# Forgetting attention: six heads' probabilities turned by VectorE and two transfers instead of by TensorE

## The chip, the cores and the metric

The kernel runs on one core of a Trainium2 chip. The metric is the device time of one execution in microseconds. Engines in the profile: PE (TensorE matmuls) and PEld (its weight loads), DVE (VectorE), ACT (ScalarE), POOL (GpSimd), SP (the queue that issues most transfers).

## The reference

A trunk of two layers over 256 tokens of width 1024, all in float32. Each layer has a half-step SwiGLU block, a token mixer, another half-step SwiGLU block, and a gated embedding. The mixer of layer 0 is a latent attention; that of layer 1, which the change concerns, is a forgetting attention with eight heads of 128:

```python
def fox_mixer(u, w_in, b_f, w_o):
    q, k, v, f_logit = jnp.split(u @ w_in, [hd, 2 * hd, 3 * hd], axis=-1)
    log_f = jax.nn.log_sigmoid(f_logit + b_f)
    cum = jnp.cumsum(log_f, axis=1).transpose(0, 2, 1)
    # per block of 128 queries [q0, q1), keys [0, q1):
    s = einsum('bqhd,bkhd->bhqk', q, k) * scale + cum[query] - cum[key]
    probs = softmax(where(k_pos <= q_pos, s, NEG_INF))
    o = einsum('bhqk,bkhd->bqhd', probs, v)
    return o.reshape(b, s, hd) @ w_o
```

With 256 tokens there are two blocks of queries; the first sees 128 keys, the second 256. So a head has three squares of 128x128 probabilities.

## The kernel before

Everything is written in an order fixed by hand; each engine runs its instructions in that order and waits for others by semaphores. The stream of the residual stands as `hT`, features on partitions and tokens along the row. Products with weights run in halves of float32: the class `Weights` fetches raw weight blocks of 512 KB in the order of a plan (`fetch`, L92, issued on SP's queue, four raw buffers), ScalarE makes the high half (`high`, L101) and VectorE the low half (`low`, L105), after which the raw buffer is free and SP may issue the next fetch. `part` (L252, L253) multiplies such a block.

`fox` first makes the values `v` for all heads, then calls `attention` with a lag of 2. The loop there runs over steps h = 0 to 9, and in step h it does, in this order:

- `shares(h - 2)`: VectorE scales the probabilities of head h-2 by the inverse of their sum (L525 to L527); then `low()` makes low halves of earlier outputs (L233);
- `project(h, 0)`: TensorE multiplies a weight block for queries (eight pairs of L252 and L253), VectorE scales it out of PSUM (L857), GpSimd adds the halves, then `W.pump()` runs one L105 and so frees a raw buffer;
- `turn(h - 2)`: TensorE transposes the three squares of probabilities into PSUM (L533), ScalarE copies them to `ptS` (L535);
- `scores(h - 1)`: TensorE (L864, L867), then VectorE's masked maxima (L506) and ScalarE's exponentials (L518, L519);
- `project(h, 1)`: the same for keys (VectorE adds, L858);
- `values(h - 2)`: TensorE multiplies `ptS` and `v` (L540, L541), ScalarE copies to `os` (L542).

From step 8 on there is nothing to project, and `fill_some` puts in pairs of the output projection, as many as `FOX_FILLS` says (4, 7, 6, 5), over the heads that `ready` counts as done. The tile `kqv` is shared by both attentions; the forgetting attention uses 16 of the 24 blocks of its part `kq`.

Of the kernel before, what the change touches and what calls it, by code (L numbers as in the profile page):

```python
# [11 lines left out]
F32 = mybir.dt.float32  # L12
# [7 lines left out]
P = 128  # L20
D = 1024
T = 256
# [3 lines left out]
H = 8  # L26
# [5 lines left out]
FOX_SCALE = 128.0 ** -0.5  # L32
# [16 lines left out]
FOX_FILLS = {(8, 0): 4, (8, 1): 7, (9, 0): 6, (9, 1): 5}  # L49
# [95 lines left out]
def trunk(ctx, tc, xT, xt, pT, pos, freq, bf, lead0, lead1, ffn_in, ffn_out, w_down, w_uq, w_ukv, mla_o,  # L145
          fox_qk, fox_v, fox_o, ple_gate, ple_proj, ple_rows, gain_row, out):
    nc = tc.nc
# [4 lines left out]
    work = ctx.enter_context(tc.tile_pool(name="work", bufs=2))  # L152
    psum = ctx.enter_context(tc.tile_pool(name="psum", bufs=7, space=bass.MemoryType.PSUM))
    dram = ctx.enter_context(tc.tile_pool(name="dram", bufs=1, space=bass.MemoryType.DRAM))
# [45 lines left out]
    ready = const.tile([P, 2], F32, name="ready")  # L200
# [21 lines left out]
    def bank(name, shape=(P, 2, T)):  # L222
        return psum.tile(list(shape), F32, name=name, tag="mm")
# [8 lines left out]
    def rest(hi, lo, src):  # L232
        nc.vector.tensor_sub(lo, src, hi.bitcast(F32))  # L233
# [21 lines left out]
    def parts(ps):  # L255
        return [ps] if len(ps.shape) == 2 else [ps[:, 0, :], ps[:, 1, :]]
# [232 lines left out]
            pass  # L489


    def attention(project, score, v, mask, scale, nxt, lag, fills, early, cumq=None):
        late = lag > 2
        os = act.tile([P, H, 2, T], F32R, name="os", tag="u")
        probs = {}
        turned = {}
        lows = []

        def scores(h):
            ps = bank("psc", (P, 3 * P))  # L500
            score(h, (ps[:, :P], ps[:, P:]))
            m = work.tile([P, 2], F32, name="m", bufs=3)
            pr = work.tile([P, 3 * P], F32, name="pr", bufs=4)

            for i, a in enumerate((slice(0, P), slice(P, 3 * P))):
                nc.vector.tensor_tensor_reduce(pr[:, a], ps[:, a], mask[:, P - i * P:], 1.0, NEG, op0=ALU.add,  # L506
                                               op1=ALU.max, accum_out=m[:, i:i + 1])
            nm = work.tile([P, 2], F32, name="nm", bufs=3)
            if cumq is None:
                nc.vector.scalar_tensor_tensor(nm, m, -1.0, scale, op0=ALU.mult, op1=ALU.mult)  # L510
                by = scale[:, 0:1], scale[:, 1:2]
            else:
                by = scale, scale
                top = work.tile([P, 2], F32, name="top", bufs=3)
                nc.vector.scalar_tensor_tensor(top, m, scale, cumq[:, h, :], op0=ALU.mult, op1=ALU.add)
                nc.vector.tensor_sub(nm, cumq[:, h, :], top)
            den = work.tile([P, 2], F32, name="den", bufs=3)
            nc.scalar.activation(pr[:, :P], pr[:, :P], AF.Exp, bias=nm[:, 0:1], scale=by[0], accum_out=den[:, 0:1])  # L518
            nc.scalar.activation(pr[:, P:], pr[:, P:], AF.Exp, bias=nm[:, 1:2], scale=by[1], accum_out=den[:, 1:2])  # L519
            probs[h] = pr, den  # L520

        def shares(h):
            pr, den = probs[h]
            inv = work.tile([P, 2], F32, name="inv", bufs=3)
            nc.vector.reciprocal(inv, den)  # L525
            nc.vector.tensor_scalar(pr[:, :P], pr[:, :P], inv[:, 0:1], None, op0=ALU.mult)
            nc.vector.tensor_scalar(pr[:, P:], pr[:, P:], inv[:, 1:2], None, op0=ALU.mult)  # L527

        def turn(h):
            pr, _ = probs.pop(h)  # L530
            pt = bank("pt", (P, 3 * P))
            for i in range(3):
                nc.tensor.transpose(pt[:, i * P:(i + 1) * P], pr[:, i * P:(i + 1) * P], ident)  # L533
            turned[h] = work.tile([P, 3 * P], F32, name="ptS", bufs=3)
            nc.scalar.activation(turned[h], pt, AF.Copy)  # L535

        def values(h):
            p = turned.pop(h)
            po = bank("po", (P, T))
            nc.tensor.matmul(po, v[:, 0, h * P:(h + 1) * P], p[:, :T], start=True, stop=False)  # L540
            nc.tensor.matmul(po[:, P:], v[:, 1, h * P:(h + 1) * P], p[:, T:], start=False, stop=True)  # L541
            nc.scalar.activation(os[:, h, 0, :], po, AF.Copy)  # L542
            lows.append((os[:, h, 0, :], os[:, h, 1, :], po))

        def low():

            while lows:
                rest(*lows.pop())


        ws, pss, upto = {}, {}, {}
        ready = 0

        def fill(d, n):
            if d not in ws:
                ws[d], = W.get()

                pss[d] = bank("ps2", (P, 2, T) if d < KD - 3 else (P, T))
            if upto.setdefault(d, 0) < n:
                part(pss[d], ws[d], os, range(upto[d], n), H - 1)  # L560
                upto[d] = n

        def fill_some(n):
            while n > 0:
                d = min(ws, key=lambda d: (upto[d], d), default=None)
                if d is None or upto[d] >= ready:
                    if len(ws) == early:
                        return
                    d = len(ws)
                    upto[d] = 0  # L570
                m = min(ready - upto[d], n)
                if m <= 0:
                    return
                fill(d, upto[d] + m)
                n -= m

        def finish(d):
            W.done(ws[d])
            src = hT[:, d, :]
            for p in parts(pss[d]):  # L580
                nc.vector.tensor_add(src, p, src)
            if d >= KD - 2:
                nxt.last(d, src)
                if d == KD - 1:
                    W.pump(2)
                return
            nxt.high(d, src)
            if d < early and d:
                nxt.low(d - 1, hT[:, d - 1, :])
            if d >= early - 1:  # L590
                W.pump()
                nxt.low(d, src)
            nxt.square(src)

        for h in range(H + lag):
            if 0 <= h - 2 < H:
                shares(h - 2)
            low()
            if h == H and not late:
                W.pump()  # L600
            if late:

                ready = h - lag - 1
            if h < H:
                project(h, 0)
            fill_some(fills.get((h, 0), 0))
            if 0 <= h - lag:
                turn(h - lag)
            if late and h in MLA_HIGHS:
                W.begin()  # L610
            if 0 <= h - 1 < H:
                scores(h - 1)
            if h < H:
                project(h, 1)
            if not late:
                W.catch_up()
            elif h in MLA_LOWS:
                W.pump(ahead=0)
            ready = h - lag - late
            fill_some(fills.get((h, 1), 0))  # L620
            if 0 <= h - lag:
                values(h - lag)
            if h >= H and not late:
                W.catch_up()
        low()
        for n in (H - 1, H):
            for d in range(early):
                fill(d, n)
                if n == H:
                    finish(d)  # L630
        for d in range(early, KD):
            fill(d, H)
            finish(d)

    def keys_values():

        kqv = big.tile([P, 2 * KF, T], F32, name="kqv", tag="big")
        return kqv[:, :24, :], kqv[:, 24:32, :].rearrange("p (t c) n -> p t (c n)", t=2), kqv[:, 32:34, :]
# [130 lines left out]
    def fox(norm, nxt):  # L769
        kq, v, _ = keys_values()  # L770
# [3 lines left out]
        cumq = work.tile([P, H, 2], F32, name="cumq", bufs=1)  # L774
# [45 lines left out]
        for c in range(3):  # L820
# [22 lines left out]
            for t in range(2):  # L843
                r = norm.rtok[:, t:t + 1]
# [6 lines left out]
        def project(h, half):  # L851
# [7 lines left out]
            if (h, half) != (H - 1, 1):  # L859
                W.pump()  # L860

        def score(h, dst):
            for t in range(2):
                nc.tensor.matmul(dst[t], kq[:, 2 * h, t * P:(t + 1) * P], kq[:, 2 * h + 1, :(t + 1) * P],  # L864
                                 start=t == 0, stop=False)
            for t in range(2):
                nc.tensor.matmul(dst[t], pick[:, h:h + 1].to_broadcast([G, P]), drop[:, :(t + 1) * P],  # L867
                                 start=False, stop=t == 1)

        attention(project, score, v, cmask[:, 1, :], FOX_SCALE, nxt, 2, FOX_FILLS, 4, cumq=cumq)  # L870


    class Embedding:
# [198 lines left out]
    for k in range(KD):  # L1072
        if k % 2 == 0:
            hi, lo = W.pair()
        c = slice(k % 2 * 4 * P, (k % 2 + 1) * 4 * P)
        n0.high(k, steps[:, k, :T], vector=k == 0)

        n = 4 * P if k else 2 * P
# [33 lines left out]
    cmask = const.tile([P, 2, 2 * P], BF16, name="cmask")  # L1112
# [103 lines left out]
    for i in range(2):  # L1216
# [6 lines left out]
        p = Embedding(i)  # L1223
# [91 lines left out]
```

## Time and profile before

| | |
|---|---|
| median of 3 runs | 988.9 us (988.71 to 989.48) |
| span of the profiled execution, first to last instruction | 987.5 us |
| TensorE, VectorE, ScalarE, GpSimd busy | 99%, 74%, 52%, 43% of the span |
| granted TensorE clock, mean | 0.998 |
| memory read | 179.65 MB, 183 GB/s over the span |
| the eight steps with projections in the forgetting attention | about 686 to 741 us |
| shares of the core's transfer engines there | 0.44 to 0.77 busy |

A span is not quite an execution's own time: 988.9 as measured against 987.5 here, and the 1.4 us around the span hold no instruction of the engines. In rows of a timeline the columns are start, duration (both in us), engine, line, operation, output and inputs, size, count, and in brackets the idle time before it and what ended it. TensorE's matmuls are pipelined, so a pitch is read from start to start, not from a duration. "To landing" is the time from the issue of a transfer to its completion.

### The profile page before, as it was taken

Reading aid. Unit: us, or ns where it says so; the run is one execution under the profiler, and the core shown is the slowest. Engines: PE = TensorE matmul, PEld = TensorE weight load, DVE = VectorE, ACT = ScalarE, POOL = GpSimd, SP = SyncE. Lnnn points to the kernel's source line nnn. Section 1 sums busy time; section 2 is a strip of 40 time slices with the busy share of each in tenths; the row PEclk is TensorE's granted clock in tenths of the full one; section 3 lists DMA queues with packets and bytes.
Section 4 is the critical chain, followed back from the end, with each engine's and each line's share of the span. In section 5 each row is a group of like instructions: output and inputs, shape, how many; then the busy total and the mean of one; then the engine's idle time right before and its main releaser. Section 6 shows DMA issues by size and latency. Waiting matters only on the chain.

```text
span 987.5 us, 15908 instructions
## 1 busy us (share of the span) xinstructions
PE 978.5 (99%) x5800; PEld 863.9 (87%) x5800; DVE 734.1 (74%) x1101; ACT 510.6 (52%) x802; POOL 423.7 (43%) x359
## 2 busy tenths in 40 slices
PE   9999999999999999999999999999999999999997
PEld 7888888998988888889888888899889888888886
DVE  6777879686858777667877886667877677786685
ACT  7555444466545554545555544546445555554361
POOL 0777731110357775111477772211221377772010
PEclk9999999999999999999999999999999999999999
DMA  8576666573456666665376665657543556666582
GB/s 326 184 253 206 200 176 198 176 209 108 147 148 208 209 210 177 203 194 185 115 209 208 195 185 178 187 178 231 157 138 101 197 182 208 209 190 199 138 278 58
DMA packets 62622, 184.11 MB, mean 186 GB/s; under 512 B 15148, under 2 KB 16816, under 8 KB 62416
## 3 DMA queue, kind: packets, MB, share of 16 engines
q1 hardware_dynamic: 61616, 181.58, 59.6%
q8 instruction: 46, 0.75, 0.3%
q10 hardware_dynamic: 576, 0.85, 0.3%
q0 software_dynamic: 352, 0.66, 0.3%
q14 instruction: 32, 0.26, 0.1%
HBM read 179.65 MB, written 1.05 MB: 183 GB/s over the span
## 4 chain that ended last, share of the span: by engine, by line
PE 94%; DVE 3%; ACT 1%; DMA 1%; issue 1%; POOL 0%; POOLq 0%; SPq 0%; ACTq 0%; DVEq 0%
PE po L252 17%; PE pu L252 16%; PE pg L252 16%; PE po L253 8%; PE pg L253 8%; PE pu L253 8%; PE ps L252 5%; PE ps L253 2%; PE ps L237 2%; PE ps L239 2%; PE ps L238 2%; DVE wlo L105 1%; PE pv L237 1%; PE pv L239 1%; PE pv L238 1%; PE po L540 1%
## 5 line engine op out<-in xcount | busy, mean ns | idle before, releaser
L105 DVE TENSOR_TENSOR wlo<-raw,whi 128x1024 fp32r<-128x1024 f32 (+2 forms) x339 | 416.2, 1235 | 28.3 <-ACT whi L101 28.1
L101 ACT ACTIVATE whi<-raw 128x1024 fp32r<-128x1024 f32 (+2 forms) x339 | 336.2, 1023 | 38.8 <-DMA raw<-in_ffn_in_dram 16.4
L395 POOL TENSOR_TENSOR gu<-two 128x256 f32<-128x256 f32 x176 | 216.7, 1232 | 114.2 <-DVE two L393 107.6
L252 PE MATMUL pg<-u,whi 128*128 128x512 f32 x702 | 251.0, 395 | 0.2 <-DVE u L297 0.2
L252 PE MATMUL pu<-u,whi 128*128 128x512 f32 x702 | 250.9, 395 | 0.1
L252 PE MATMUL po<-hs,whi 128*128 128x512 f32 x704 | 246.8, 394 | 0.0
L253 PE MATMUL pg<-u,wlo 128*128 128x256 f32 x702 | 197.1, 281 | 0.6 <-DVE wlo L105 0.4
L253 PE MATMUL po<-hs,wlo 128*128 128x256 f32 x704 | 197.2, 280 | 0.0
L253 PE MATMUL pu<-u,wlo 128*128 128x256 f32 x702 | 196.8, 280 | 0.0
L252 PEld LDWEIGHTS po<-hs,whi 128*128 128x128 f32 x704 | 132.2, 188 | 31.3
L252 PEld LDWEIGHTS pu<-u,whi 128*128 128x128 f32 x702 | 131.8, 188 | 31.3 <-issue 0.4
L252 PEld LDWEIGHTS pg<-u,whi 128*128 128x128 f32 x702 | 131.8, 188 | 31.1 <-ACT whi L1080 0.3
L253 PEld LDWEIGHTS pg<-u,wlo 128*128 128x128 f32 x702 | 132.0, 188 | 1.6 <-DVE wlo L105 1.1
L253 PEld LDWEIGHTS po<-hs,wlo 128*128 128x128 f32 x704 | 132.3, 188 | 0.0
L253 PEld LDWEIGHTS pu<-u,wlo 128*128 128x128 f32 x702 | 132.0, 188 | 0.1
L413 POOL TENSOR_TENSOR hid<-sg,gu 128x256 f32<-128x256 f32 x88 | 122.1, 1387 | 6.9
L308 POOL TENSOR_TENSOR acc<-acc,sq 128x256 f32<-128x256 f32 x42 | 43.3, 1031 | 177.7 <-ACT sq L303 155.0
L229 ACT ACTIVATE hs<-hid 128x256 fp32r<-128x256 f32 x88 | 36.8, 418 | 155.2 <-POOL hid L413 153.1
L233 DVE TENSOR_TENSOR hs<-hid,hs 128x256 fp32r<-128x256 f32 x88 | 53.7, 610 | 72.4 <-ACT hs L229 72.4
L292 ACT ACTIVATE u<-state 128x256 fp32r<-128x256 f32 x47 | 24.0, 512 | 119.9 <-DVE state L472 99.5
L393 DVE TENSOR_TENSOR two<-pg,rb 128x512 f32<-128x512 f32 x88 | 60.1, 683 | 27.6 <-PE pg L253 18.4
L472 DVE SCALAR_TENSOR_TENSOR state<-po,state 128x256 f32<-128x256 f32 x64 | 27.1, 424 | 58.5 <-PE po L253 57.3
(264 smaller groups left out, 1163.3 us busy)
## 6 DMA issues: line engine op xcount, KB each, us to landing
raw<-in_ffn_in_dram SPq DMA_DIRECT2D x172, 512.0 KB, 4.2
raw<-in_ffn_out_dram SPq DMA_DIRECT2D x64, 512.0 KB, 4.0
raw<-in_ffn_out_dram SPq DMA_DIRECT2D x32, 384.0 KB, 3.3
raw<-in_fox_qk_dram SPq DMA_DIRECT2D x16, 512.0 KB, 4.4
raw<-in_mla_o_dram SPq DMA_DIRECT2D x8, 512.0 KB, 4.6
raw<-in_ple_gate_dram SPq DMA_DIRECT2D x8, 512.0 KB, 4.6
raw<-in_fox_o_dram SPq DMA_DIRECT2D x8, 512.0 KB, 3.5
raw<-in_ple_rows_dram SPq DMA_DIRECT2D x8, 512.0 KB, 4.5
```

What stands on the lines that cost most here:

```text
L101: self.nc.scalar.activation(self.pairs[i][0][:, c], self.raws[i][:, c], AF.Copy)
L105: self.nc.vector.tensor_sub(lo[:, c], self.raws[i][:, c], hi[:, c].bitcast(F32))
L229: nc.scalar.activation(hi, src, AF.Copy)
L233: nc.vector.tensor_sub(lo, src, hi.bitcast(F32))
L237: nc.tensor.matmul(ps, w[0], x[0], start=first, stop=False)
L238: nc.tensor.matmul(ps, w[1], x[0], start=False, stop=False)
L252: nc.tensor.matmul(ps, hi, x[:, k], start=k == 0, stop=False)
L253: nc.tensor.matmul(ps[:, 1, :], lo, x[:, k, 0, :], start=False, stop=k == last)
L308: nc.gpsimd.tensor_add(new, self.acc, sq)
L393: nc.vector.tensor_mul(two, ps, norm.rb2)
L395: nc.gpsimd.tensor_add(gu[c, i], two[:, 0, :], two[:, 1, :])
L413: nc.gpsimd.tensor_mul(hid[c], gu.pop((c, 0)), gu.pop((c, 1)))
```

## The change

For heads 0 to 5 (`moved = 6`) the transposition goes another way. In `shares`, VectorE transposes all 32x32 squares of the head's 128x384 probabilities (L531) into one of two buffers in the unused blocks of `kqv`. Transposing squares leaves each square in the wrong place among partitions; four transfers on SP's queue, one for each group of 32 partitions, write them to a place in memory, `keys`, so that rows there are keys (L536). In the same step, behind `project(h, 0)`, `back` reads `keys` into `ptS` with one transfer (L541). TensorE's three transposes and ScalarE's copy are gone for these heads, and their values stand a step later: values of head h-3 behind `project(h, 0)`, ahead of the scores. They read `ptS` in pieces of 32 columns, as the squares lie. Heads 6 and 7 are turned by TensorE as before. `ready` counts one head less while heads come later.

The text of the change:

```diff
--- before.py
+++ after.py
@@ -489,7 +489,7 @@
             pass
 
 
-    def attention(project, score, v, mask, scale, nxt, lag, fills, early, cumq=None):
+    def attention(project, score, v, mask, scale, nxt, lag, fills, early, cumq=None, moved=0, room=None):
         late = lag > 2
         os = act.tile([P, H, 2, T], F32R, name="os", tag="u")
         probs = {}
@@ -525,6 +525,21 @@
             nc.vector.reciprocal(inv, den)
             nc.vector.tensor_scalar(pr[:, :P], pr[:, :P], inv[:, 0:1], None, op0=ALU.mult)
             nc.vector.tensor_scalar(pr[:, P:], pr[:, P:], inv[:, 1:2], None, op0=ALU.mult)
+            if h < moved:
+                pr, _ = probs.pop(h)
+                squares = room[h % 2]
+                nc.vector.transpose(squares.rearrange("p (k u c) -> p k u c", k=4, u=3),
+                                    pr.rearrange("p (u k c) -> p k u c", u=3, k=4))
+                turned[h] = dram.tile([P, 3 * P], F32, name="keys", bufs=2)
+                to = turned[h].rearrange("(k r) (q n) -> q r k n", k=4, q=4)
+                for q in range(4):
+                    nc.sync.dma_start(to[q], squares[q * 32:(q + 1) * 32, :].rearrange("r (k n) -> r k n", k=4))
+
+        def back(h):
+
+            p = work.tile([P, 3 * P], F32, name="ptS", bufs=3)
+            nc.sync.dma_start(p, turned[h])
+            turned[h] = p
 
         def turn(h):
             pr, _ = probs.pop(h)
@@ -537,8 +552,15 @@
         def values(h):
             p = turned.pop(h)
             po = bank("po", (P, T))
-            nc.tensor.matmul(po, v[:, 0, h * P:(h + 1) * P], p[:, :T], start=True, stop=False)
-            nc.tensor.matmul(po[:, P:], v[:, 1, h * P:(h + 1) * P], p[:, T:], start=False, stop=True)
+            if h < moved:
+                p = p.rearrange("p (q u c) -> p u q c", q=4, u=3)
+                p = p[:, :2], p[:, 2]
+                to = po.rearrange("p (u q c) -> p u q c", u=2, q=4)
+                to = to, to[:, 1]
+            else:
+                p, to = (p[:, :T], p[:, T:]), (po, po[:, P:])
+            nc.tensor.matmul(to[0], v[:, 0, h * P:(h + 1) * P], p[0], start=True, stop=False)
+            nc.tensor.matmul(to[1], v[:, 1, h * P:(h + 1) * P], p[1], start=False, stop=True)
             nc.scalar.activation(os[:, h, 0, :], po, AF.Copy)
             lows.append((os[:, h, 0, :], os[:, h, 1, :], po))
 
@@ -604,7 +626,11 @@
             if h < H:
                 project(h, 0)
             fill_some(fills.get((h, 0), 0))
-            if 0 <= h - lag:
+            if 0 <= h - lag < moved:
+                back(h - lag)
+            if 0 <= h - lag - 1 < moved:
+                values(h - lag - 1)
+            if moved <= h - lag:
                 turn(h - lag)
             if late and h in MLA_HIGHS:
                 W.begin()
@@ -616,9 +642,9 @@
                 W.catch_up()
             elif h in MLA_LOWS:
                 W.pump(ahead=0)
-            ready = h - lag - late
+            ready = h - lag - (late or 0 < h - lag <= moved)
             fill_some(fills.get((h, 1), 0))
-            if 0 <= h - lag:
+            if moved <= h - lag:
                 values(h - lag)
             if h >= H and not late:
                 W.catch_up()
@@ -859,6 +885,9 @@
             if (h, half) != (H - 1, 1):
                 W.pump()
 
+        squares = kq[:, 16:24, :].rearrange("p (i s) n -> p i (s n)", i=2)[:, :, :3 * P]
+        squares = squares[:, 0], squares[:, 1]
+
         def score(h, dst):
             for t in range(2):
                 nc.tensor.matmul(dst[t], kq[:, 2 * h, t * P:(t + 1) * P], kq[:, 2 * h + 1, :(t + 1) * P],
@@ -867,7 +896,7 @@
                 nc.tensor.matmul(dst[t], pick[:, h:h + 1].to_broadcast([G, P]), drop[:, :(t + 1) * P],
                                  start=False, stop=t == 1)
 
-        attention(project, score, v, cmask[:, 1, :], FOX_SCALE, nxt, 2, FOX_FILLS, 4, cumq=cumq)
+        attention(project, score, v, cmask[:, 1, :], FOX_SCALE, nxt, 2, FOX_FILLS, 4, cumq=cumq, moved=H - 2, room=squares)
 
 
     class Embedding:
```

What it moves, in three places. First TensorE in step 3, from the end of the first half projection (`ps`, from input `u` and weight halves `whi`, `wlo`) to the scores (`psc`); `pt` and `ptS` are turned probabilities, `po` a head's output. Before:

```order
L252 MATMUL ps_7736<-u_4934,whi_7545 128x512
L253 MATMUL ps_7736<-u_4934,wlo_7546 128x256
L533 MATMUL pt_7762<-ident_87,pr_7691 128x128 x3
L864 MATMUL psc_7768<-kqv_7261 128x128
L864 MATMUL psc_7768<-kqv_7261 128x256
```

Now:

```order
L252 MATMUL ps_7739<-u_4934,whi_7545 128x512
L253 MATMUL ps_7739<-u_4934,wlo_7546 128x256
L562 MATMUL po_7767<-ptS_7685,kqv_7261 128x256
L563 MATMUL po_7767<-ptS_7685,kqv_7261 128x128
L893 MATMUL psc_7771<-kqv_7261 128x128
L893 MATMUL psc_7771<-kqv_7261 128x256
```

The turn of head 1 is gone, and values of head 0 stand in its place; they stood at the end of step 2 before.

Then SP's queue in steps 3 and 4, where `raw` are fetches of weights. Before:

```order
L92 DMA raw_7647<-in_fox_qk_dram 128x1024
L92 DMA raw_7677<-in_fox_qk_dram 128x1024
L92 DMA raw_7725<-in_fox_qk_dram 128x1024
L92 DMA raw_7760<-in_fox_qk_dram 128x1024
L92 DMA raw_7808<-in_fox_o_dram 128x1024
```

Now:

```order
L92 DMA raw_7727<-in_fox_qk_dram 128x1024
L536 DMA keys_7734<-kqv_7261 32x4x96 x4
L92 DMA raw_7763<-in_fox_qk_dram 128x1024
L541 DMA ptS_7765<-keys_7734 128x384
L92 DMA raw_7811<-in_fox_o_dram 128x1024
L536 DMA keys_7818<-kqv_7261 32x4x96 x4
L92 DMA raw_7848<-in_fox_o_dram 128x1024
L541 DMA ptS_7850<-keys_7818 128x384
```

In each step the four writes have come in between two fetches, and the read stands behind the second of them; it waits for all four writes.

Last VectorE at the start of step 6, with the probabilities `pr` of head 4. Before:

```order
L525 RECIPROCAL inv_7980<-den_7947 128x2
L526 TENSOR_SCALAR pr_7940<-pr_7940,inv_7980 128x128
L527 TENSOR_SCALAR pr_7940<-pr_7940,inv_7980 128x256
L233 TENSOR_TENSOR os_7524<-po_7976,os_7524 128x256
L857 TENSOR_TENSOR two_8002<-ps_7985,rb_7347 128x512
```

Now:

```order
L525 RECIPROCAL inv_7983<-den_7954 128x2
L526 TENSOR_SCALAR pr_7947<-pr_7947,inv_7983 128x128
L527 TENSOR_SCALAR pr_7947<-pr_7947,inv_7983 128x256
L531 STREAM_TRANSPOSE kqv_7261<-pr_7947 128x384
L233 TENSOR_TENSOR os_7524<-po_7937,os_7524 128x256
L883 TENSOR_TENSOR two_8011<-ps_7994,rb_7347 128x512
```

The transposition of squares has come in behind the scaling, ahead of the low half of an earlier head's output and of the scaling of the half projection.

## The prediction

> **What bounds the kernel now.** I read the page first: the busy shares and the shares of the chain that ended last.
>
> ```profile
> span 987.5 us, 15908 instructions
> PE 978.5 (99%) x5800; PEld 863.9 (87%) x5800; DVE 734.1 (74%) x1101; ACT 510.6 (52%) x802; POOL 423.7 (43%) x359
> PE 94%; DVE 3%; ACT 1%; DMA 1%; issue 1%; POOL 0%; POOLq 0%; SPq 0%; ACTq 0%; DVEq 0%
> ```
>
> TensorE is busy for 99% of the span and carries 94% of the chain. So an instruction taken from it is a gain of its full pitch, and a microsecond in which it waits is lost in full; work on the other engines counts only where TensorE ends up waiting for it. The median of the runs is 988.9, 1.4 above this span; I take that 1.4 as fixed and add my differences to the median.
>
> Next the chain in order of time, for the price of what is removed (first and second of the eight turns of this attention; the next four read 0.33 each):
>
> ```profile
> 699.26 0.61 PE pt L533 x3
> 706.94 0.33 PE pt L533 x3
> ```
>
> Then TensorE's timeline through one step, from values (L540) of one step to those of the next:
>
> ```profile
> 703.35 0.59 PE L540 MATMUL po<-ptS,kqv 128*128 128x256 f32 x2
> 703.92 0.48 PE L252 MATMUL ps<-u,whi 128*128 128x512 f32 x1
> 704.24 0.28 PE L253 MATMUL ps<-u,wlo 128*128 128x256 f32 x1
> 706.43 0.39 PE L252 MATMUL ps<-u,whi 128*128 128x512 f32 x1
> 706.78 0.49 PE L533 MATMUL pt<-ident,pr 128*128 128x128 f32 x3
> 707.11 0.82 PE L864 MATMUL psc<-kqv 128*128 128x128 f32 x4
> 707.85 0.48 PE L252 MATMUL ps<-u,whi 128*128 128x512 f32 x1
> 710.76 0.59 PE L540 MATMUL po<-ptS,kqv 128*128 128x256 f32 x2
> 714.22 0.49 PE L533 MATMUL pt<-ident,pr 128*128 128x128 f32 x3
> ```
>
> Between turns lie 714.22 - 706.78 = 7.44 us without a gap: turn 0.33, scores 0.74, and each half of the projection eight pairs of L252 and L253, 0.35 each (706.43 to 706.78). The first pair after other matmuls takes about 0.09 more (L252 to L253 is 0.32 at 703.92). Half a projection alone is 8 x 0.35 = 2.80; after scores 2.89; values with the slow pair behind them 0.57 + 0.09 = 0.66.
>
> VectorE's timeline of the same stretch shows how soon the probabilities of a head are ready (L527) and what comes behind:
>
> ```profile
> 703.55 0.69 DVE L857 TENSOR_TENSOR two<-ps,rb 128x512 f32<-128x512 f32 x1 [1.48 <-PE ps L253]
> 704.62 1.22 DVE L105 TENSOR_TENSOR wlo<-raw,whi 128x1024 fp32r<-128x1024 f32 x1
> 706.15 0.35 DVE L527 TENSOR_SCALAR pr<-pr,inv 128x256 f32<-128x256 f32 x1
> 706.41 0.42 DVE L233 TENSOR_TENSOR os<-po,os 128x256 fp32r<-128x256 f32 x1
> 707.05 0.69 DVE L857 TENSOR_TENSOR two<-ps,rb 128x512 f32<-128x512 f32 x1 [0.21 <-PE ps L253]
> 707.66 1.22 DVE L105 TENSOR_TENSOR wlo<-raw,whi 128x1024 fp32r<-128x1024 f32 x1
> 710.96 0.69 DVE L857 TENSOR_TENSOR two<-ps,rb 128x512 f32<-128x512 f32 x1 [1.15 <-PE ps L253]
> ```
>
> VectorE idles 0.21 + 1.15 us in a step, both times waiting for TensorE. I count time below from t0, the end of the second half projection on TensorE (703.35 here); the probabilities are ready at 706.15 + 0.35 = 706.50, t0 + 3.15.
>
> **What is removed.** Six turns on TensorE: 0.61 + 5 x 0.33 = 2.26 us, all on the path (the 0.61 includes 0.28 in which TensorE waited for the first probabilities, which goes too). The six ScalarE copies out of PSUM go as well; ScalarE was not on the path there, so they are worth nothing.
>
> **What is added on VectorE.** One block transpose of 128x384 per head. Nearest rows:
>
> ```profile
> L887 DVE STREAM_TRANSPOSE rows<-state x8: 432/439/440, 900.6 to 955.6; 128x256 f32<-128x256 f32 x8
> L346 DVE STREAM_TRANSPOSE turned<-wide x4: 245/246/314, 199.7 to 775.2; 128x64 f32<-128x64 f32 x3, 128x128 f32<-128x128 f32 x1
> ```
>
> From 0.246 at 64 columns and 0.439 at 256, about 0.001 a column, 384 columns give 0.57 (bounds 0.44 and 0.74, three times 0.246). The idle 1.36 us of a step covers it: L857 behind it starts some 0.3 later, and the 1.15 ahead of the next one shrinks. Cost nothing; with 1.36 used up it would be the excess. The squares are ready at t0 + 3.15 + 0.03 + 0.57 = 3.75, and the first write can issue at t0 + 3.8.
>
> **What is added on SP's queue.** Per head four writes to memory (32 partitions, runs of 384 bytes, 48 KB each) and one read of 192 KB, in one queue with the fetches of weights. Today's fetches there, and the rows that come nearest to the new transfers:
>
> ```profile
> 705.87 3.39 SPq L92 DMA_DIRECT2D raw<-in_fox_qk_dram  x2
> L92 SPq DMA_DIRECT2D raw<-in_fox_o_dram x8: 327/328/328, 713.3 to 738.7; - x8
> DMA to landing us min/median/max: 3.5/3.5/4.3
> 924.23 10.54 SPq L896 DMA_DIRECT2D rows<-rows  x16
> DMA to landing us min/median/max: 1.9/2.0/3.0
> L996 SPq DMA_DIRECT2D out_dram<-fin x3: 335/357/378, 980.2 to 983.9; - x3
> DMA to landing us min/median/max: 2.0/2.3/2.5
> p_sb<-in_pT_dram ACTq DMA_DIRECT2D x2, 256.0 KB, 2.6
> ```
>
> The landing line behind each group is that group's: 3.5 for the fetches of this stretch (705 to 740), 2.0 for the sixteen moves of squares between 924 and 936, 2.3 for the stores of the output.
>
> Issue: the sixteen moves took 10.54 / 16 = 0.66 us each on SP, the stores 0.36. The new writes have the moves' 32 partitions and several short runs in each, so I take 0.66 and keep 0.36 for the range. Last write issues at t0 + 3.8 + 3 x 0.66 = 5.78, SP is free at 6.44. Landing: 2.0, so the last write has landed at 7.8. The moves behind that 2.0 stay on chip, though, and the stores (2.3) have long runs; the only short runs written to memory today are these, issued by GpSimd:
>
> ```profile
> L348 POOL DMA_DIRECT2D row<-turned x4: 624/630/753, 200.3 to 775.7; - x4
> DMA to landing us min/median/max: 1.8/4.2/4.8
> ```
>
> I keep 2.0, since the new writes share SP's queue and pattern with the moves, and 4.2 as the upper end. The Trainium skill (DMA: Bandwidth & Descriptors, Anatomy of one DMA) says that most of a transfer's fixed cost is waiting for the target's write receipt, and "This can cause a surprisingly long delay especially when the write target is HBM"; its Specifications add that runs under 512 bytes are done by read-modify-write, without a price. The row with 4.2 agrees with the first; the stores' 2.3 does not, and no run here shows the second. By the rows that I take the sum comes to the value below; by a late receipt it would be the first rival's.
>
> The fetch that stands between writes and read is set free by L105: 707.66 + 1.22, plus the 0.3 of shift, is t0 + 5.85, but SP issues it only at 6.44, and it lands 3.5 later, at 9.94. The read issues at about 7.9. On its own it would take some 2.3 (between 2.0 for a store and 2.6 for 256 KB), to 10.2. But it stands behind the fetch in one queue, and in the second batch of moves, issued behind fetches, waiting of that sort shows:
>
> ```profile
> L896 SPq DMA_DIRECT2D rows<-rows x6: 597/608/618, 957.6 to 960.9; - x6
> DMA to landing us min/median/max: 5.1/5.5/5.9
> ```
>
> 5.5 instead of 2.0. So the read lands after the fetch, by what its own bytes need: 512 KB take 3.5 and 256 KB 2.6, which makes 0.67 for 192 KB an upper bound, and I take 0.5. That is 10.44, with 0.06 for the wake-up of TensorE L = t0 + 10.5.
>
> **When TensorE wants it.** In the new order values of head h-3 stand in step h right after the first half projection. From t0 of a head to its values there lie: 2.80, values of the head before 0.66, scores 0.74, 2.89, 2.80 = 9.89. For head 0 no values lie between: 9.23. For head 5 the last half projection is replaced by four pairs of the output projection (from 741.07 to the turn at 742.59 before, with the slow first pair):
>
> ```profile
> 741.07 0.48 PE L252 MATMUL ps<-os,whi 128*128 128x512 f32 x1
> 742.59 0.49 PE L533 MATMUL pt<-ident,pr 128*128 128x128 f32 x3
> ```
>
> so 9.89 - 2.80 + 1.40 = 8.49. A wait of the head before gives the next one as much time. So with L = 10.5: head 0 waits 1.27; head 1 needs 11.16 and waits nothing; head 2 waits 0.61, head 3 nothing, head 4 0.61, head 5 10.5 - 8.49 - 0.61 = 1.40. Together 3.89. **Sum:** 3.89 - 2.26 = +1.6 us, 988.9 + 1.6 = 990.5. For L above 9.89 the sum is 3 L - 29.87: each tenth of a microsecond in the transfers counts 0.3.
>
> What else moves: the fetch is 0.6 later on SP and the one of the next half waits for nothing (the read has issued by 7.9, that fetch is released near t0 + 9.5). I cost this at nothing; the cover is that the list of waits between 693 and 757 has no wait of ScalarE or VectorE on a fetched tile, and that VectorE's waits are for TensorE:
>
> ```profile
> DVE two L857 <- PE ps L253: 9.8, 13, 1.5
> ```
>
> Without that cover each late fetch would hold L105 and with it L857. The output projection's filling in steps 8 and 9 is dealt out in another order (one block opened earlier since one head fewer is ready) with the same number of pairs, 4, 7, 6, 5 and 6: nothing.
>
> **Rivals.**
>
> Writes to memory that land late (slower), as the 4.2 of L348 has it. With 4.2 the last write lands at 5.78 + 4.2 = 9.98, the read issues at 10.1 and lands 2.3 later: L = 12.5, sum +7.6, 996.5. It decides from a landing of about 2.4 us: then the read is no longer behind the fetch but bound by the writes, L passes 10.62 and the sum +2.0. For it: the median, and that a fetch is mostly in flight. Against: another queue, another issuing engine, and one of the four took 1.8.
>
> Transfers hidden anyway (faster). With SP at 0.36 a write, the last one issues at 4.88 and lands at 6.9; the fetch goes at 5.85 and lands at 9.35, the read at 9.85: L = 9.9, the waits are 0.67, 0, 0, 0, 0 and 1.41 (with rounding), the sum -0.1 to -0.2, 988.8. If moreover the read is not held by the fetch, L is about 9.0, the only wait is head 5's 0.5, and the sum -1.7; all six hidden, -2.26 and 986.6, needs L of 8.5 or less, less than any rows give. For it: VectorE and the queue have slack everywhere. Against: the 5.5 above.
>
> **How the numbers follow.** A measurement here tells about 0.2% (2.0 us) from no change: faster means under 986.9, slower over 990.9. Transfers as priced or somewhat better, L between 8.6 and 10.62, which stays within 0.2%: 0.50, and the likeliest value is 990.5. Writes or read later than L = 10.62: 0.38. Everything hidden, L under 8.6: 0.10 (no rows give that, but a turn may be worth more than its 0.33; with L = 9.9 each turn would have to give 0.65). The remaining 0.02, a late weight, I add to the middle. The range: from L = 9.2 (only head 5 waits, 0.7, sum -1.5: 987.4) to L = 11.7 (sum +5.2: 994.1).
>
> **What would show it.** In the changed profile: no turn at TensorE's row of heads 0 to 5; the first write some 0.65 us behind VectorE's last scaling of a head; writes 0.66 apart on SP; 2.0 to their landing; the read landing behind the fetch. TensorE should wait at values for the transfer, at heads 0, 2, 4 and 5 with about 1.3, 0.6, 0.6 and 1.4, and almost not at 1 and 3. It is wrong if the waits are missing (L under 9), if all six show (another work shifts t0), if VectorE is named as the releaser of the waits, or if weights are.

## The result, and the profile after

The changed kernel takes 992.88 us (median of 5 runs, 992.01 to 994.98); the kernel before took 988.9 in the same comparison. The ratio is 1.0041 (95%: 1.003 to 1.0053): slower, by about 4 us. That is the side that had a chance of 0.38; the time lies inside the range, 2.4 us above the forecast. Among the executions of the experiments below, the profiled one of "the transfers alone" had a granted clock of 0.692 and took 1299.79 us; it is left out, so that kernel has no trace to read.

The page of the changed kernel, in the same lines as before:

```profile
span 990.9 us, 15935 instructions
PE 977.5 (99%) x5782; PEld 862.6 (87%) x5782; DVE 735.7 (74%) x1107; ACT 507.7 (51%) x796; POOL 424.1 (43%) x359
PE 91%; DVE 4%; DMA 2%; ACT 1%; issue 1%; SPq 0%; POOL 0%; POOLq 0%; ACTq 0%; DVEq 0%
```

TensorE has 18 matmuls fewer and is busy 1.0 us less, yet the span is 3.4 us longer, and its share of the chain fell from 94% to 91%. VectorE and transfers took the place. The chain in order of time shows how, at head 0 and at head 4 (start, duration, what; "DMA" rows run from the issue to the landing):

```profile
699.16 0.59 DVE kqv L531
699.77 0.34 SPq L536
...
701.12 2.48 DMA keys<-kqv
703.73 2.85 DMA ptS<-keys
706.72 0.67 PE po L562 x2
...
730.96 3.58 DMA keys<-kqv
734.62 3.86 DMA ptS<-keys
738.62 0.67 PE po L562 x2
```

(Left out are the other writes' issues.) Block transpose, four writes, the last one's landing, the read's landing, and then values. No weight and no VectorE wait stands between. TensorE's timeline has values at these rows (the first of heads 0 to 4), with the scores ahead of head 0's:

```profile
698.79 0.82 PE L893 MATMUL psc<-kqv 128*128 128x128 f32 x4
706.72 0.67 PE L562 MATMUL po<-ptS,kqv 128*128 128x256 f32 x2 [1.32 <-DMA ptS<-keys]
713.91 0.70 PE L562 MATMUL po<-ptS,kqv 128*128 128x256 f32 x2
721.31 0.67 PE L562 MATMUL po<-ptS,kqv 128*128 128x256 f32 x2
728.48 0.66 PE L562 MATMUL po<-ptS,kqv 128*128 128x256 f32 x2
738.62 0.67 PE L562 MATMUL po<-ptS,kqv 128*128 128x256 f32 x2 [2.88 <-DMA ptS<-keys]
```

The bracket shows a wait only where the profile sees TensorE empty; short waits have to be read from the pitch. A step in which nothing waits takes 7.09 us in the new order (rows of the two-steps-later kernel below), and from the scores of one step to the place of head 0's values in the next lie 6.46 (in that kernel, which has no values there, from scores at 698.60 to scores at 705.06). So the waits, as pitch beyond these, are 706.72 - 698.79 - 6.46 = 1.47 at head 0, then 0.10, 0.31, 0.08 at heads 1 to 3, and 10.14 - 7.09 = 3.05 at head 4; head 5 has none. Together 5.0, against 2.26 saved: the attention costs 2.7 us. That accounts for 2.7 of the span's 3.4. The other 0.7 is made of small shifts elsewhere, a wait of 0.54 for GpSimd near 958 among them, which the repeat below does not have.

The new transfers, by line in the stretch of the attention (issue time min/median/max in ns; then each group's own landing line, over the transfers whose landing the profile can tell from the others', 12 of the 24 writes here):

```profile
L536 SPq DMA_DIRECT2D keys<-kqv x24: 303/426/450, 699.8 to 737.9; - x24
...
DMA to landing us min/median/max: 1.8/2.9/4.5
...
L541 SPq DMA_DIRECT2D ptS<-keys x6: 337/338/338, 703.7 to 740.8; - x6
...
DMA to landing us min/median/max: 2.9/3.1/3.9
```

### The profile page after: what moved, and what is told of

Same layout as the page of the kernel before. It is cut to its first block, busy times and chain, and to the rows that moved or that the text cites. A ratio compares the mean times of both kernels' runs of the same rounds, so it can differ in the third digit from the quotient of the medians.

```text
span 990.9 us, 15935 instructions
## 1 busy us (share of the span) xinstructions
PE 977.5 (99%) x5782; PEld 862.6 (87%) x5782; DVE 735.7 (74%) x1107; ACT 507.7 (51%) x796; POOL 424.1 (43%) x359
## 4 chain that ended last, share of the span: by engine, by line
PE 91%; DVE 4%; DMA 2%; ACT 1%; issue 1%; SPq 0%; POOL 0%; POOLq 0%; ACTq 0%; DVEq 0%
PE pg L252 16%; PE pu L252 16%; PE po L252 16%; PE pg L253 8%; PE pu L253 8%; PE po L253 8%; PE ps L252 4%; PE ps L253 2%; DVE wlo L105 2%; PE ps L237 2%; PE ps L239 1%; PE ps L238 1%; PE po L562 1%; PE pv L237 1%; PE pv L239 1%
## 5 line engine op out<-in xcount | busy, mean ns | idle before, releaser
L233 DVE TENSOR_TENSOR hs<-hid,hs 128x256 fp32r<-128x256 f32 x88 | 53.6, 609 | 72.5 <-ACT hs L229 72.5
```

## The experiments

**The same kernel again** (no edit), to see which waits come back.

> The changed kernel once more, for a second profile. Theory A (TensorE waits at the values for the read from memory, and the length of each wait hangs on what else the transfer engines carry just then): again 2 to 6 us slower than before, but the two waits of the first profile (1.32 us at head 0, 2.88 us at head 4) need not have these sizes; head 0 waits again, since no values of an earlier head give it time, and the others may. Theory B (the waits are fixed by the order alone): the same two waits at the same heads within 0.2 us.

Measured: 992.07 us against 989.81, ratio 1.0028 (1.0017 to 1.0038). TensorE's rows of the heads that waited:

```profile
707.16 0.67 PE L562 MATMUL po<-ptS,kqv 128*128 128x256 f32 x2 [1.42 <-DMA ptS<-keys]
737.03 0.67 PE L562 MATMUL po<-ptS,kqv 128*128 128x256 f32 x2 [0.93 <-DMA ptS<-keys]
743.67 0.67 PE L562 MATMUL po<-ptS,kqv 128*128 128x256 f32 x2 [0.73 <-DMA ptS<-keys]
```

By pitch the waits are 1.57, 0.07, 0.23, 0.09, 1.12 and 0.95: sum 4.0. Head 0 waits as before; head 4 waits less, and head 5, no longer covered by head 4's long wait, waits instead. Theory A holds: the same cause, with other sizes.

**Values two steps later**, which takes the waits away and leaves everything else:

```diff
-            if 0 <= h - lag - 1 < moved:
-                values(h - lag - 1)
+            if 0 <= h - lag - 2 < moved:
+                values(h - lag - 2)
...
-            ready = h - lag - (late or 0 < h - lag <= moved)
+            ready = h - lag - (late or (2 if 0 < h - lag <= moved + 1 else 0))
```

> The values of heads 0 to 5 stand two steps later than before, not one. Theory A (the waits are the whole loss): no wait of TensorE for a read is left; what remains is the saving of the turns, of which the first profile shows about 0.26 us a step, 1.5 us in all: 987.4 us, 0.15% faster than before, at best 986.6. Theory B (the transfers cost time elsewhere: late weights, VectorE's longer steps, crowded memory): the waits go, others take their place, and the time stays 2 us or more above before.

Measured: 989.17 us, ratio 0.9996 (0.9987 to 1.0005). TensorE's rows of two unwaited steps, and of the wait that is new; then VectorE's low halves (L233) that end it:

```profile
718.58 0.59 PE L562 MATMUL po<-ptS,kqv 128*128 128x256 f32 x2
719.01 0.38 PE L563 MATMUL po<-ptS,kqv 128*128 128x128 f32 x2
725.67 0.59 PE L562 MATMUL po<-ptS,kqv 128*128 128x256 f32 x2
749.72 0.50 PE L252 MATMUL ps<-os,whi 128*128 128x512 f32 x1 [1.26 <-DVE os L233]
```

```profile
748.91 0.76 DVE L233 TENSOR_TENSOR os<-po,os 128x256 fp32r<-128x256 f32 x2 [2.82 <-ACT os L564]
```

No wait for a read is left, and the pitch is 725.67 - 718.58 = 7.09, which is 0.35 under the 7.44 of before: the turns are worth what the prediction said. So the waits were the loss, as theory A has it, but its 987.4 us were missed: 1.26 us comes back at the output projection. `low()` takes the list of finished heads from its end, so the low half of head 5 is queued on VectorE behind that of head 7 and waits for the last values of all, though its own were multiplied 2.5 us earlier (745.10 against 747.64).

**The same, with the low halves in the order of writing:**

```diff
-                rest(*lows.pop())
+                rest(*lows.pop(0))
```

> Values two steps later, and the low halves of finished heads taken in the order in which the values were written down (first in, first out), not last in, first out. Theory A (the 1.26 us gap ahead of the output projection's pairs with heads 5 and 6, seen when values came two steps later, is head 5's low half queued on VectorE behind that of head 7, whose values end last): the gap is gone or under 0.2 us, TensorE waits for no read, and the time is 1.0 to 1.3 us below that of values two steps later, which is 1.7 to 2.2 us below before: ratio 0.998 (0.9975 to 0.999). Theory B (the gap is the length of the chain from the last values over ScalarE and VectorE to TensorE, whichever low half goes first): the gap moves a few rows down and stays above 0.8 us; ratio 0.9995 to 1.000.

Measured: 987.73 us against 989.82, ratio 0.9981 (0.9972 to 0.999). VectorE's low halves, and TensorE's last values with the row behind them:

```profile
746.91 0.42 DVE L233 TENSOR_TENSOR os<-po,os 128x256 fp32r<-128x256 f32 x1 [0.28 <-ACT os L564]
749.42 0.42 DVE L233 TENSOR_TENSOR os<-po,os 128x256 fp32r<-128x256 f32 x1 [2.09 <-ACT os L564]
```

```profile
748.15 0.59 PE L562 MATMUL po<-ptS,kqv 128*128 128x256 f32 x2
...
748.73 0.48 PE L252 MATMUL ps<-os,whi 128*128 128x512 f32 x1
```

Head 5's low half now runs at 746.91, head 7's alone at 749.42, and TensorE goes on without a gap. Theory A holds. The edit also reorders the low halves of the latent attention, but the gain does not come from there: the first scores of the forgetting attention stand at 692.70 here and at 692.59 before. From them to the last pair of the output projection (766.50 before, 764.26 here) it takes 71.56 us in place of 73.91, which is 2.35 less, all of the 2.26 that the turns are worth. This is the version that beats both kernels, by 2 us against before.

**The order alone:** TensorE turns the six heads, nothing is written or read, values a step later.

```diff
-            if h < moved:
-                pr, _ = probs.pop(h)
-                ...
-            if 0 <= h - lag < moved:
-                back(h - lag)
...
-            if moved <= h - lag:
+            if 0 <= h - lag:
                 turn(h - lag)
```

> The order of the change alone: TensorE turns the six heads as before, with no block transposes and no transfers, but their values stand a step later, ahead of the scores. Theory A (the change's cost is in the waits for reads): as before, ratio 0.9995 to 1.0005, no new gap over 0.3 us on TensorE between 690 and 757 us. Theory B (the order itself costs, for example by low halves or the output projection's filling coming late): 1.001 to 1.002, with waits for VectorE or ScalarE at the output projection.

Measured: 989.49 us against 989.82, ratio 0.9996 (0.9987 to 1.0005), and TensorE's gaps in the stretch sum up to 0.06 us, as before. Theory A holds: the order costs nothing.

**The transfers alone:** order and turns of before, with the transposes, writes and reads added; the read goes to a tile that nobody uses.

```diff
-            p = work.tile([P, 3 * P], F32, name="ptS", bufs=3)
-            nc.sync.dma_start(p, turned[h])
-            turned[h] = p
+            p = work.tile([P, 3 * P], F32, name="ptU", bufs=1)
+            nc.sync.dma_start(p, placed.pop(h))
```

> The order and the turns on TensorE of before; VectorE's block transposes, the four writes and the read of each of the six heads are added, but the read goes into a tile that nobody uses, so that only their use of VectorE, SP and the transfer engines is left. Theory A (VectorE, SP and the transfer engines have slack): ratio 1.000 to 1.0005, no wait for a weight, fetches land at most 1 us later. Theory B (late weights cost too): 1.001 to 1.003, with TensorE waiting for wlo or whi between 700 and 745 us.

Measured: 989.88 us against 989.82, ratio 1.0 (0.9991 to 1.0009). VectorE, SP and the transfer engines have room for the new work; whether fetches land later there, no trace tells. So the cost needs both halves: the transfers, and values that wait for them.

**The read ahead of the fetch in SP's queue:**

```diff
+            if 0 <= h - lag < moved:
+                back(h - lag)
             if h < H:
                 project(h, 0)
             fill_some(fills.get((h, 0), 0))
-            if 0 <= h - lag < moved:
-                back(h - lag)
```

> In SP's queue the read of the probabilities stands ahead of the weight fetch of the same step, so that it has no fetch in front of it. Theory A1 (the read is late because it stands behind that fetch, as predicted): reads land in 2.0 to 2.3 us instead of 2.7 to 3.9, waits shrink by 0.6 us or more at head 0, and the time falls to 988 to 990.5 us. Theory A2 (the read is late because of its own landing and of the writes' before it): reads still take 2.7 us or more, the waits stay within 0.3 us, 991 to 995 us. Theory B: the fetch now goes out later by the landing of the writes, about 2 us, and a wait for weights shows up.

Measured: 991.66 us, ratio 1.0016 (1.0008 to 1.0025). Landing of the writes (first group) and of the reads:

```profile
L536 SPq DMA_DIRECT2D keys<-kqv x24: 302/428/469, 700.0 to 738.0; - x24
...
DMA to landing us min/median/max: 2.3/3.6/4.3
...
L541 SPq DMA_DIRECT2D ptS<-keys x6: 337/338/338, 703.7 to 741.2; - x6
...
DMA to landing us min/median/max: 2.2/2.3/2.3
```

The read lands in 2.3 instead of 3.1, as priced "on its own". But the fetch that had stood ahead of it now issues later and meets the next head's writes, which land in 3.6 instead of 2.9. The gain of 0.8 in one leg is given back in the other (0.7); gaps of 0.58, 0.76, 0.96 and 0.88 remain at heads 0, 1, 4 and 5. By pitch the waits sum up to 4.1 against the repeat's 4.0. So theory A1 is right on the read and on head 0's wait (0.74 by pitch, 1.57 in the repeat), and its time was missed; no wait for a weight shows up.

**The writes on ScalarE's queue**, so that no fetch stands ahead of them in their own queue:

```diff
-                    nc.sync.dma_start(to[q], ...)
+                    nc.scalar.dma_start(to[q], ...)
...
             if 0 <= h - lag < moved:
+                send(h - lag)
                 back(h - lag)
```

> The changed kernel with the four writes of each head issued on ScalarE's queue, ahead of its copy of the values (where ScalarE idles by 2 us and more a step), so that no fetch of weights stands ahead of them in their queue; the read stays on SP behind the fetch. Theory A (the writes land late because the fetch of 512 KB ahead of them in SP's queue has its packets ahead of theirs): they land 1.8 to 2.3 us after issue at heads 0 to 5 (2.6 to 4.5 with SP's queue), and the read issues 0.5 to 1 us earlier; TensorE's waits for reads shrink to 2 us or less in sum, ratio to before 0.999 to 1.0015. Theory B (the transfer engines are simply shared: a fetch in flight slows the writes wherever they are queued): they land 2.4 us or more after issue at most heads, the waits stay at 3.5 us or more, ratio 1.002 to 1.004.

Measured: 994.16 us against 989.73, ratio 1.0045 (1.0032 to 1.0059). The writes by line:

```profile
L540 ACTq DMA_DIRECT2D keys<-kqv x24: 309/446/1444, 699.7 to 738.6; - x24
...
DMA to landing us min/median/max: 1.7/3.1/4.3
```

A median of 3.1 against 2.9: no better, and the repeat on SP's queue has 2.6. Of theory B this much is shown: the place in SP's queue is not what makes the writes late. The Trainium skill (DMA: Bandwidth & Descriptors, Issuing engines are not separate DMA queues) says that, whatever engine issues, transfers run on the same 16 transfer engines and interleave there. This run agrees, with 3.1 beside 2.9.

That it is the 512 KB in flight is supported by rows, but no run here has these writes with no fetch just ahead. Head 2's last write in the changed kernel was the quickest, 1.78: it was issued at 716.17, when the one fetch ahead of it (713.57) had 0.8 us left. With two fetches ahead, at 712.38 and 713.10, it took 3.05 in the kernel that reads first; it was issued there at 715.71, with 2.3 us left of the second.

The waits by pitch are 1.9, 0, 0.7, 0.1, 3.1 and 0.4 here, 6.2 in sum, above the 5.0 of the first profile, and the ratio lies above theory B's range. The rounds from first write to read now take 4.89, 5.52, 6.67 and 5.79 us at heads 0, 1, 4 and 5, where SP's queue had 3.96, 3.92, 5.17 and 4.21; why they got longer is not shown.

**Values that read their probabilities in one piece** (it multiplies the squares as they lie, without putting them in place):

```diff
-            if h < moved:
+            if h < 0:
                 p = p.rearrange("p (q u c) -> p u q c", q=4, u=3)
```

> Values of heads 0 to 5 read the probabilities as contiguous rows of 256 and 128 columns, not in pieces of 32; the queries are then in another order, so this leaves the right placing out. Theory A (pieces cost TensorE time): the pitch from the first values matmul to the second falls from 0.51 us to the 0.43 of before, 0.08 a head, 0.5 us in all, inside the scatter of the waits. Theory B (the 0.51 comes from something else, such as a wait just ahead): the pitch stays 0.51.

Measured: 991.43 us, ratio 1.0018 (1.0009 to 1.0027); the repeat, in the same comparison, has 1.0028 (1.0017 to 1.0038), and the intervals overlap. TensorE's values at a head where it did not wait:

```profile
713.68 0.60 PE L562 MATMUL po<-ptS,kqv 128*128 128x256 f32 x2
714.11 0.38 PE L563 MATMUL po<-ptS,kqv 128*128 128x128 f32 x2
```

0.43 from L562 to L563, as in the two-steps-later kernel, which reads in pieces (718.58 to 719.01): the pieces of 32 columns cost nothing. The 0.51 of the changed kernel (706.72 to 707.23 and the like) is a matmul behind a wait; in one piece it is the same 0.51 there (706.55 to 707.06).

This trace shows something else, at head 4. Its wait is longer than any in the other traces, and behind it the granted clock (third column from the right in the view by windows) is halved:

```profile
738.87 1.19 PE L562 MATMUL po<-ptS,kqv 128*128 128x256 f32 x2 [3.35 <-DMA ptS<-keys]
738.80:742.20 3.40, 3.33 (x11) 2.81 (x12) 0.07 (x1) 0.38 (x1) 0.15 (x1) 0.50 0.70 197
```

From these values to the second pair of the next half projection it takes 3.52 us (738.87 to 742.39), and 1.90 in the changed kernel's first profile (738.62 to 740.52), where TensorE's idle time of 2.88 was followed by the full clock. So this one wait cost another 1.6 us.

**TensorE's instruction fetch moved by one step.** At head 4 the first profile has this among the transfers from 729 to 735 (throughput in 40 slices of 0.15 us; queues q8 and q14 fetch instructions):

```profile
GB/s 27 191 109 137 164 218 328 328 328 355 410 410 294 158 166 194 230 146 206 128 218 100 10 18 18 13 10 8 10 21 21 218 55 191 82 328 273 273 218 410
q8 instruction: 1, 0.02, 1.4%
q14 instruction: 1, 0.01, 0.3%
keys<-kqv SPq DMA_DIRECT2D x4, 48.0 KB, 4.4
```

From about 732.3 to 733.7 next to nothing moves. A transfer of 16 KB on q8 began at 731.4 and took 1.35 us. The execution has 46 of these, some 21 us apart, one for about 250 of TensorE's 11564 matmuls and weight loads. To move it by one step, 84 instructions of TensorE were put at the start of the kernel:

```diff
     for _ in range(16):
         nc.tensor.matmul(cold, warm[:, :P], warm, start=True, stop=True)
+    for _ in range(42):
+        nc.tensor.matmul(cold[:, :64], warm[:, :P], warm[:, :64], start=True, stop=True)
```

> The changed kernel with 42 more small matmuls at the very start (84 instructions of TensorE, as many as one step of the attention has), so that TensorE's instruction fetches of 16 KB, one for 256 of its instructions, come one step earlier in the stream: at about 724 us instead of 731 (counted without the later start). Theory A (that fetch holds head 4's writes and the fetch around them, so that they land 3.6 to 4.5 us after their issue): head 3's writes now land 3.3 us or more after issue and its values wait for the read, 0.6 us or more by pitch; head 4's writes land in 2.4 to 3.0. Theory B (something else at head 4, such as the other instruction fetch of 8 KB or SP's slow issue): head 3's writes still land in 1.7 to 2.5 and head 4's in 3.0 to 4.5. The total is not to be compared: the added matmuls lengthen the start by up to 4 us.

Measured: 992.71 us against 989.82, ratio 1.0039 (1.0024 to 1.0055). The fetch on q8 comes at 724.4 now. SP's timeline of heads 3 and 4, first of the changed kernel, then of this one (four writes, the fetch, and the read that issues when the last write has landed):

```profile
722.09 1.77 SPq L536 DMA_DIRECT2D keys<-kqv  x4
725.22 0.34 SPq L541 DMA_DIRECT2D ptS<-keys  x1
...
728.18 0.33 SPq L92 DMA_DIRECT2D raw<-in_fox_o_dram  x1
729.45 1.92 SPq L536 DMA_DIRECT2D keys<-kqv  x4
731.49 1.63 SPq L92 DMA_DIRECT2D raw<-in_fox_o_dram  x1
734.62 0.34 SPq L541 DMA_DIRECT2D ptS<-keys  x1
```

```profile
722.03 1.80 SPq L536 DMA_DIRECT2D keys<-kqv  x4
726.49 0.34 SPq L541 DMA_DIRECT2D ptS<-keys  x1
...
729.51 1.93 SPq L536 DMA_DIRECT2D keys<-kqv  x4
731.54 0.54 SPq L92 DMA_DIRECT2D raw<-in_fox_o_dram  x1
733.03 0.34 SPq L541 DMA_DIRECT2D ptS<-keys  x1
```

From first write to read, head 4 went from 5.17 to 3.52 and head 3 from 3.13 to 4.46: the delay moved with the fetch, as theory A has it, while the fetch on q14 stayed (731.8 and 731.4). The other traces with the writes on SP's queue say the same. In six of them a fetch on q8 falls into head 4's round, which takes 4.49 to 5.17, and head 3's without one takes 3.13 to 3.43. Head 0 meets a fetch on q8 in this run alone, at 701.2: 4.38, and 3.75 to 3.96 in the others. The size was less than expected at head 3: only the last of its four writes was late (3.04), the wait 0.36 instead of 0.6 or more. And the waits in sum did not fall below the repeat's, since head 4 no longer gives head 5 cover:

```profile
706.82 0.67 PE L562 MATMUL po<-ptS,kqv 128*128 128x256 f32 x2 [1.70 <-DMA ptS<-keys]
743.39 0.67 PE L562 MATMUL po<-ptS,kqv 128*128 128x256 f32 x2 [1.57 <-DMA ptS<-keys]
```

By pitch the waits are about 1.9, 0.1, 0.3, 0.4, 0 and 1.8: sum 4.4, against the repeat's 4.0.

## Why the prediction was right or wrong

- **What bounds the kernel, and what the turns are worth:** right. The pitch fell by 0.35 (7.44 to 7.09) where 0.33 was taken, and the kernel without waits gained 2.35 in the attention where 2.26 was forecast.
- **VectorE's block transpose:** 0.59 at 699.16, against 0.57. It cost nothing, as said, and so did the rest of the added work (transfers alone: 1.0) and the new order (0.9996).
- **Issue on SP:** wrong row. 0.66 was taken from the moves on chip; the writes took 0.43 (median 0.426), nearer to the stores' 0.36 kept for the range. The last write issues at t0 + 5.1, not 5.78.
- **"Landing: 2.0":** wrong row as well, in the other direction. The writes take 2.9 in the median (2.6 in the repeat). The last write of head 0 landed 2.48 after its issue, at t0 + 7.6, where 7.8 was forecast: the two errors cancelled. The view that would have said so stood in the prediction for the read alone, the moves of squares issued behind fetches: 5.5 instead of 2.0. The writes stand behind a fetch too (728.18 at head 4, with its writes 1.3 us later), and I priced them as if the engines were free. That the fetch is the reason is supported, not shown (see the writes on ScalarE's queue).
- **"Behind the fetch":** the effect is right, 3.1 in place of 2.3, and 2.3 again with the read ahead of the fetch. Its working is right in part: the read was to land 0.5 behind the fetch, and did so at heads 2 and 3 (0.59 and 0.48), but at head 0 it took 1.20 (705.39 to 706.59), with the fetch 0.5 earlier than forecast (t0 + 9.4, not 9.94). For the writes a place in another queue does not help (3.1 beside 2.9).
- **L = t0 + 10.5:** head 0's read landed at 706.59 = t0 + 10.6 (t0 at 696.0), by errors that cancelled, as said. The prediction names no row for its 0.06 for TensorE's wake-up; from this landing to the values at 706.72 it took 0.13. For the other heads t0 is taken as 3.8 ahead of their first write: head 5 has 10.6, right too; head 1's 11.4 is covered by head 0's wait; heads 2 and 3 have 10.1 and 10.0, which is why head 2 waits 0.31 and not 0.61.
- **Waits of 1.27, 0, 0.61, 0, 0.61, 1.40:** repeat 1.57, 0.07, 0.23, 0.09, 1.12, 0.95, shifted kernel 1.9, 0.1, 0.3, 0.4, 0, 1.8. The sums of 4.0 and 4.4 stand beside a forecast of 3.89; less the 2.26 that makes +1.8 and +2.1, against +1.6. The sum is nearer than its parts, and that is partly luck: neither run is free of a meeting with an instruction fetch, at head 4 (4.49 from first write to read) and at head 3 (4.46). The first profile has 5.0, for the 3.05 at head 4.
- **Where the number failed:** L was taken as one value for all heads. Head 4's was 12.8 in the first profile (10.9 in the repeat, 10.0 with the fetch moved). The prediction's 1.6 lacked a term for a head that meets an instruction fetch: 3.05 in place of 0.61 + 1.40, one microsecond more. That and the 0.7 us outside the attention are the 1.8 by which the profiled difference of 3.4 exceeds the forecast's 1.6. The repeat's ratio, 1.0028, lies nearer to the forecast's 1.0016, though its interval (1.0017 to 1.0038) leaves it just out.
- **The rivals:** late writes in the form named, 4.2 at every head and 996.5, did not come; it was the right mechanism with less than half its price, 0.9 over the 2.0 instead of 2.2. Hidden transfers came only when values stood two steps later.

What stays open is the spread between executions of one kernel (992.0 to 995.0), as only single ones have a trace. One thing on record goes with it. In the changed kernel, its repeat and the four experiments whose values still wait for reads, 8 of 43 executions took over 994 us. Their mean granted clock is 0.995 to 0.997, and that of the other 35 is 0.997 to 0.999. The one of the eight that has a trace is that of values in one piece, where an idle time of 3.35 us was followed by half the clock for 3.4 us; half the clock for so long lowers the mean by 0.0017, by calculation. That the other seven had such a wait is likely, and not shown.

## What to carry to other kernels

A round trip through memory beside a stream of weights costs what its transfers take with the stream in flight: here 2.4 to 2.9 for a small write (medians of six traces) and 3.1 for the read, not the 2.0 and 2.3 of the rows that they were priced from. Give the consumer the spare of a whole step: TensorE wanted the reads at t0 + 9.89 and they landed at 10.0 to 12.8, so that every delay counted. A second step, together with the low halves in order, turned +4 us into -2. And when a consumer moves, look at what hangs on its order further down: here a list taken from its end held 1.26 of the gain until it was taken from its front.

## What the runs showed of the hardware that was not expected

- A fetch of 16 KB for TensorE's instructions, every 21 us or so, delays the transfers beside it: head 4's round from first write to read took 4.49 to 5.17 us with it in six traces, 3.52 without it. Such meetings moved by one step with 84 more of TensorE's instructions ahead.
- Behind an idle time of 3.35 us TensorE was granted half its clock for 3.4 us, which cost another 1.6 us; behind idle times of 2.88 and 2.97 in two other traces the clock was full. A long wait for a transfer can thus cost more than its own length.
- In the same places issuing slowed: SP's fetch took 1.63 us at 731.49 where 0.54 and 0.35 stand in other rows, and one of ScalarE's writes 1.44 us. With the instruction fetch moved to 701.2, the slow fetch at head 0 took 1.11 us at 701.35 (0.62 and 0.46 in the changed kernel and the repeat). So slow issuing went along with the instruction fetch; by what way is not shown.
- Writes of 48 KB in runs of 384 bytes issue in 0.43 us, between the 0.33 of a fetch and the 0.66 of moves on chip.
